# A two-layer decoder step on one core: four output blocks half by half, and the next norm's scales behind the first group's products

## The chip, the cores and the metric

The kernel runs on one core of a Trainium2 chip. The metric is the device time of one execution in microseconds (us). The engines are named as in the profile: PE is TensorE (matmuls), PEld its weight load, DVE VectorE, ACT ScalarE, POOL GpSimd and SP SyncE, which here only issues transfers.

## The reference

One inference step of a decoder with two layers, on 576 tokens (a prompt of 512 and 8 samples of 8), model width 1024, hidden width 2816. Each layer has three sublayers, and every sublayer lies between two RMS norms:

```
x += 0.5 * post_f1(SwiGLU_1(pre_f1(x)))
x += post_m(mixer(pre_m(x) @ W_in) @ W_out)
x += 0.5 * post_f2(SwiGLU_2(pre_f2(x)))
rmsnorm(x, g) = x * rsqrt(mean(x*x) + EPS) * g
```

The mixer of layer 0 ("even") is a gated delta rule beside a short convolution, that of layer 1 ("odd") is sparse attention over a paged cache beside a gated MLP. Outputs are x and the new states and cache rows.

## The kernel before

Activations lie transposed: model rows on 128 partitions in KC = 8 chunks, tokens along the columns, in two halves: half 0 has 256 columns, half 1 has 320 (HALF, HW). Every weight and every activation is split into a high and a low part in the type fp32r (`split`, L98: the high part is a cast on ACT, L101, the low part a subtraction on DVE, L102), and one product of a 128x128 weight block takes three matmuls (`mm3`, L118): whi with the high activation (L119), whi with the low (L120), wlo with the high (L121). Weights come in tiles of eight blocks, 512 KB (`weight`, L105): a transfer on the SP queue into one of three raw buffers, then the split.

The order of the sublayers is ffn(0,0), even, ffn(0,1), ffn(1,0), odd, ffn(1,1). The instructions of each engine stand in an order that the framework's scheduler makes from the program's order; each engine works its list in that order, and an instruction that waits holds all that stand behind it.

**A feed-forward sublayer** (`ffn`, L281) goes over the hidden width in two parts of 11 blocks. For each hidden block it makes the gate and the up product (8 chunks of `mm3`) for half 0 and then half 1. These use x that is not yet divided by its norm: since the scale of a token is a factor of its column, DVE multiplies it in when it takes the products out of PSUM (t, L316, and u, L317: product times r). Then come silu (ACT, L318), the product u*t and its split into hh and hl. After the 11 blocks comes the down projection: eight output blocks `mb` for each half, 33 matmuls each, in the order of `self.out_order`: the blocks 0 to 5 alternate between the halves, the blocks 6 and 7 come first for half 0 and then for half 1. In the second part DVE adds each product to y (L344), ACT squares y (L186) and DVE sums the squares (L187) for the post norm (`y_done`, L245). The mixers end likewise with `proj_out`, 24 matmuls for each output block.

**The seam between two sublayers** is `boundary(hf)` (L209), which runs when a half's last output block is done. `rstd` (L155) makes the scales of the post norm: matmuls of the summed squares with ones (PE, L161, result in the PSUM kind psm), a square root (ACT, L163 and L166), a reciprocal (DVE, L167 and L169), transposes that spread them over the partitions (PE, L173). Then, over the eight chunks, DVE makes bt = y * scale (L227) and adds it to x (L229, or L231 for the last two), ACT writes xh (L195) and DVE xl (L196) for the next sublayer, ACT squares x (L186), POOL adds the squares (L187), and x is stored (L239). From the sum on POOL comes the scale r of the next sublayer's norm by the same `rstd`, with a copy of the result to SBUF (ACT, L177).

**The first group of a sublayer** (`group`, L123) is four products: gate and up of the first two hidden blocks, or the first four blocks of a mixer's input projection. For half 0 it goes product by product, for half 1 chunk by chunk through all four. PSUM has eight banks, three of the kind g, three m and two f; `bank` (L93) hands out the g and f banks in turn, so that five products can be open. A bank is free again when DVE has multiplied its product by r. The scale r of half 0 is made at the end of its boundary; that of half 1 before the last chunk of its first group:

```
later = lambda: self.rstd(accx, w, 1.0 / D, EPS, f"r{hf}")
return later if hf else later()
```

In `odd`, 24 indirect transfers on POOL's queue gather pages of the cache (gcmp, L833, 16 times, and gsel, L858, 8 times); the first is issued after the last sum of squares of the boundary (`issue_after(self.last.ins)`).

Of the kernel before, what the change touches and what calls it, by code (L numbers as in the profile page):

```python
# [16 lines left out]
P = 128  # L17
# [21 lines left out]
class Step:  # L39
    def __init__(self, ctx, tc, a, o):  # L40
        self.tc, self.nc, self.a, self.o = tc, tc.nc, a, o
        self.n = 0
        self.turn = 0
        self.const = ctx.enter_context(tc.tile_pool(name="const", bufs=1))
        self.res = ctx.enter_context(tc.tile_pool(name="res", bufs=1))
        self.wp = ctx.enter_context(tc.tile_pool(name="wp", bufs=4))
        self.ps = ctx.enter_context(tc.tile_pool(name="ps", bufs=4, space=PSUM))
        nc = self.nc
        self.dram = ctx.enter_context(tc.tile_pool(name="dram", bufs=2, space=bass.MemoryType.DRAM))
        self.xd = [a["xT"][:, :, c0:c1] for c0, c1 in HALF]  # L50
        self.g = self.const.tile([P, 12, KC], F32, name="g")
        nc.scalar.dma_start(self.g, a["gT"])
        self.ident = self.const.tile([P, P], F32, name="ident")
        nc.scalar.dma_start(self.ident, a["ident"])
        self.ones = self.const.tile([P, P], F32, name="ones")
        nc.vector.memset(self.ones, 1.0)
        self.biases = {}
        self.small = {}
        self.out_order = [(mb, hf) for mb in range(KC - 2) for hf in range(2)]
        self.out_order += [(mb, hf) for hf in range(2) for mb in range(KC - 2, KC)]  # L60
# [44 lines left out]
    def weight(self, src, inner=P, pool=None):  # L105
        nc = self.nc
        pool = pool or self.wp
        shape = [P, 8 * P // inner, inner]
        raw = self.wp.tile(shape, F32, tag="raw", name=self.nm("raw"), bufs=3)
        bufs = 4 if pool is self.wp else 2  # L110
        hi = pool.tile(shape, F32R, tag="whi", name=self.nm("whi"), bufs=bufs)
        lo = pool.tile(shape, F32R, tag="wlo", name=self.nm("wlo"), bufs=bufs)
# [10 lines left out]
    def group(self, ws, act, rs, hf):  # L123
# [7 lines left out]
        for k in range(KC):  # L131
            if k == KC - 1:
                rs[hf] = rs[hf]()
            for (whi, wlo), p in zip(ws, ps):
                self.mm3(p[:, :w], whi[:, k, :], wlo[:, k, :], act[0][hf][:, k, :], act[1][hf][:, k, :], k == 0, k == KC - 1)
        return ps
# [8 lines left out]

    def new_act(self):
        hi, lo = [], []
        for hf in range(2):
            hi.append(self.res.tile([P, KC, HW[hf]], F32R, tag=f"xh{hf}", name=self.nm("xh")))
            lo.append(self.res.tile([P, KC, HW[hf]], F32R, tag=f"xl{hf}", name=self.nm("xl")))  # L150
        return hi, lo
# [57 lines left out]
    def boundary(self, hf, y, x, acc_y, gpost, c, gnext, act):  # L209
# [4 lines left out]
        accx = self.acc_tile("x") if gnext is not None else None  # L214
# [25 lines left out]
        if gnext is not None:  # L240
            self.xd[hf] = xd
            later = lambda: self.rstd(accx, w, 1.0 / D, EPS, f"r{hf}")
            return later if hf else later()
# [40 lines left out]
    def ffn(self, l, f, act, rs, gpost, gnext, first=None):  # L284
        nc, a = self.nc, self.a
        with ExitStack() as ctx:
# [4 lines left out]
            nact, nrs = None, [None, None]  # L291
            rs = list(rs)
            hp.tile([P, 16], F32, tag="pad", name=self.nm("pad"))
            for part in range(2):
# [27 lines left out]
                if part == 1:  # L322
                    x = self.load_x(yp)
# [5 lines left out]
                def block(n):  # L329
                    t = n // 8  # L330
                    if t not in tiles:
                        tiles[t] = self.weight(a["wdn"][l, f, part, t], pool=yp if part == 1 and t >= 9 else None)
                    return tiles[t][0][:, n % 8, :], tiles[t][1][:, n % 8, :]

                for mb, hf in self.out_order:
# [7 lines left out]
                        else:  # L343
# [4 lines left out]
                            if mb == KC - 1:  # L348
                                if nact is None and gnext is not None:
                                    nact = self.new_act()  # L350
# [4 lines left out]
    def proj_out(self, wsrc, oact, order, gpost, gnext):  # L355
        nc = self.nc
        with ExitStack() as ctx:
# [1140 lines left out]
```

## Time and profile before

| | |
|---|---|
| Median of 3 runs | 2463.08 us (2462.32 to 2464.12) |
| Profiled execution: its own time | 2465.13 us |
| Profiled execution: span of the profile | 2463.4 us |
| PE busy | 2409.8 us, 98% of the span |
| DVE, ACT, POOL busy | 51%, 38%, 7% |
| Mean granted clock of PE | 0.986 |

An engine's busy time is the time in which it has an instruction at work. The waits name the releaser: the instruction whose end let the waiting one start. "issue" means that the profile shows nothing that the engine waited for, "remote" that the releaser is not known. In a timeline the columns are the start, the duration, the engine, the line, the operation, the tile written and those read, the shape, how many instructions the row joins, and in brackets the idle time before it with its releaser. Neighbouring matmuls overlap, so a matmul's price is the distance of two starts, not its duration.

### The profile page before, as it was taken

How to read it: one execution, taken by the hardware profiler on the slowest of the kernel's cores; microseconds unless marked ns; L12 is line 12 of the kernel's file. 1: busy time of each engine (PE TensorE's matmuls, PEld its weight loads, DVE VectorE, ACT ScalarE, POOL GpSimd, SP SyncE). 2: the span in 40 equal slices, each digit the busy share in tenths (PEclk: the TensorE clock that was granted, in tenths of full speed). 3: DMA queues.
4: the chain of work that ended last, by engine and by line, in shares of the span. 5: the costliest groups of instructions: out<-in, count | busy, mean ns of one | idle time of the engine just before them, and what ended most of it. 6: DMA issues, size and time to landing. Idle time of an engine off the chain costs nothing.

```text
span 2463.4 us, 43370 instructions
## 1 busy us (share of the span) xinstructions
PE 2409.8 (98%) x18169; PEld 2318.4 (94%) x18169; DVE 1246.4 (51%) x2489; ACT 926.6 (38%) x1727; POOL 170.9 (7%) x259
## 2 busy tenths in 40 slices
PE   8999999999999999999999999998999999999998
PEld 8999999898999999999999999997866799999997
DVE  5432444777755743244474324445547646423444
ACT  5222334554324522233353223343336645222332
POOL 1000000300001200000020000006002001000000
PEclk9999999999999999999999999999889999999999
DMA  6222222301113322222332222225312123222221
GB/s 224 86 86 78 86 88 95 110 32 63 59 61 140 128 87 86 78 86 86 103 137 86 79 77 94 86 87 183 122 35 75 61 78 137 86 86 78 86 86 56
DMA packets 70323, 226.72 MB, mean 92 GB/s; under 512 B 11136, under 2 KB 17568, under 8 KB 70096
## 3 DMA queue, kind: packets, MB, share of 16 engines
q1 hardware_dynamic: 64288, 204.27, 23.9%
q0 software_dynamic: 5552, 19.57, 2.4%
q8 instruction: 143, 2.34, 0.4%
q14 instruction: 52, 0.43, 0.1%
q10 hardware_dynamic: 288, 0.11, 0.0%
HBM read 204.26 MB, written 20.72 MB: 91 GB/s over the span
## 4 chain that ended last, share of the span: by engine, by line
PE 76%; issue 17%; DVE 5%; ACT 1%; another core or an unknown queue 1%; DMA 1%; POOL 0%; POOLq 0%; DVEq 0%; SPq 0%; ACTq 0%
PE psg L119 14%; PE psg L120 14%; PE psg L121 14%; PE psf L121 8%; PE psf L120 8%; PE psf L119 8%; PE psm L1206 1%; PE psm L494 1%; PE psm L516 1%; PE psf L1248 1%; DVE xl L196 1%; PE psg L1235 1%; PE psm L514 1%; DVE x L229 1%
## 5 line engine op out<-in xcount | busy, mean ns | idle before, releaser
L119 PE MATMUL psg<-xh,whi 128*128 128x256 f32 (+1 forms) x2464 | 734.0, 298 | 11.8 <-ACT xh L195 8.3
L120 PE MATMUL psg<-xl,whi 128*128 128x256 f32 (+1 forms) x2464 | 733.5, 298 | 6.8 <-DVE xl L196 5.2
L121 PE MATMUL psg<-xh,wlo 128*128 128x256 f32 (+1 forms) x2464 | 730.3, 297 | 0.9 <-issue 0.8
L102 DVE TENSOR_TENSOR wlo<-raw,whi 128x1024 fp32r<-128x1024 f32 x330 | 405.2, 1228 | 351.5 <-ACT whi L101 350.0
L101 ACT CAST whi<-raw 128x1024 fp32r<-128x1024 f32 x330 | 345.4, 1050 | 569.2 <-PE psg L120 344.4
L119 PEld LDWEIGHTS psg<-xh,whi 128*128 128x128 f32 x2464 | 467.5, 190 | 14.5 <-ACT xh L195 9.1
L120 PEld LDWEIGHTS psg<-xl,whi 128*128 128x128 f32 x2464 | 466.6, 189 | 14.1 <-DVE xl L196 8.5
L121 PEld LDWEIGHTS psg<-xh,wlo 128*128 128x128 f32 x2464 | 466.7, 189 | 3.9 <-issue 3.0
L120 PE MATMUL psf<-xl,whi 128*128 128x320 f32 (+1 forms) x1280 | 375.8, 294 | 1.5 <-DVE xl L196 1.3
L119 PE MATMUL psf<-xh,whi 128*128 128x320 f32 (+1 forms) x1280 | 375.9, 294 | 0.5 <-ACT xh L195 0.3
L121 PE MATMUL psf<-xh,wlo 128*128 128x320 f32 (+1 forms) x1280 | 375.4, 293 | 0.3
L119 PE MATMUL psg<-hh,whi 128*128 128x256 f32 (+1 forms) x836 | 245.6, 294 | 0.0
L120 PE MATMUL psg<-hl,whi 128*128 128x256 f32 (+1 forms) x836 | 245.2, 293 | 0.0
L121 PE MATMUL psg<-hh,wlo 128*128 128x256 f32 (+1 forms) x836 | 245.1, 293 | 0.0
L120 PEld LDWEIGHTS psf<-xl,whi 128*128 128x128 f32 x1280 | 240.3, 188 | 2.6 <-DVE xl L196 2.2
L119 PEld LDWEIGHTS psf<-xh,whi 128*128 128x128 f32 x1280 | 240.5, 188 | 1.2 <-ACT xh L195 0.5
L121 PEld LDWEIGHTS psf<-xh,wlo 128*128 128x128 f32 x1280 | 240.4, 188 | 0.9 <-DVE wlo L102 0.9
L119 PE MATMUL psf<-hh,whi 128*128 128x320 f32 (+1 forms) x572 | 169.3, 296 | 0.0
L120 PE MATMUL psf<-hl,whi 128*128 128x320 f32 (+1 forms) x572 | 169.0, 295 | 0.0
L121 PE MATMUL psf<-hh,wlo 128*128 128x320 f32 (+1 forms) x572 | 168.8, 295 | 0.0
L101 ACT CAST hh<-u 128x320 fp32r<-128x320 f32 (+1 forms) x176 | 75.9, 433 | 245.7 <-DVE u L319 245.7
L187 POOL TENSOR_TENSOR acc<-acc,sq 128x320 f32<-128x320 f32 (+1 forms) x77 | 70.3, 913 | 1388.8 <-ACT sq L186 1357.7
(467 smaller groups left out, 3173.0 us busy)
## 6 DMA issues: line engine op xcount, KB each, us to landing
raw<-in_wgu SPq DMA_DIRECT2D x176, 512.0 KB
raw<-in_wdn SPq DMA_DIRECT2D x88, 512.0 KB
raw<-in_w_ein SPq DMA_DIRECT2D x28, 512.0 KB
raw<-in_w_oin SPq DMA_DIRECT2D x14, 512.0 KB
xd<-x SPq DMA_DIRECT2D x10, 640.0 KB
x<-xd POOLq DMA_DIRECT2D x10, 640.0 KB
xd<-x SPq DMA_DIRECT2D x10, 512.0 KB
x<-xd POOLq DMA_DIRECT2D x10, 512.0 KB
```

The costliest lines, as they stand in the source:

```text
L101: first = nc.scalar.copy(hi, src)
L102: nc.vector.tensor_tensor(lo, src, hi.bitcast(F32), ALU.subtract)
L119: mm(out, whi, ahi, start=first, stop=False)
L120: mm(out, whi, alo, start=False, stop=False)
L121: mm(out, wlo, ahi, start=False, stop=last)
L187: return (eng or nc.vector).tensor_tensor(acc[:, :w], acc[:, :w], sq[:, :w], ALU.add)
L196: nc.vector.scalar_tensor_tensor(lo, xs, g, hi.bitcast(F32), ALU.mult, ALU.subtract)
L229: (nc.gpsimd if gnext is None and hf and k == 0 else nc.vector).tensor_tensor(xs, xs, t, ALU.add)
L494: nc.tensor.matmul(pz[:w, i * w:i * w + w], m[:, i, :], x[:, i, :], start=True, stop=True)
L514: nc.tensor.matmul(pr[:, 1, i, :], xt[:, i, :], zt[:, i, :], start=True, stop=True)
L516: nc.tensor.matmul(pr[:, 0, i, :], zt[:, i, :], xt[:, i, :], start=True, stop=True)
L1206: nc.tensor.matmul(S[g][:, 0:L], qq[gd, j, P * i:P * i + P], kk[gd, 0:L], start=True, stop=True)
```

## The change

Five things change.

1. `out_order` is now a function. In the second part of a feed-forward sublayer and in `proj_out` the output blocks 0 to 3 alternate between the halves, and the blocks 4 to 7 come first for half 0, then for half 1. In the last sublayer half 1 is ahead of half 0, so that half 0 is the last to end. The first part of a feed-forward sublayer, behind which there is no seam, alternates throughout (`in_turn`).
2. Since the down blocks 4 to 7 are now used for half 0 and again, later, for half 1, their weights stay longer: the tiles from 7 on have buffers of their own, two in the pool yp, two in the space of the next sublayer's xh and xl of half 1 (`spare`). In `proj_out` four weights have buffers of their own rather than two.
3. `boundary` gives the making of r back for both halves, and `group` calls it after all products of the half's first group, for both halves.
4. The sum of squares of half 0's x uses the buffers of accy.
5. The pad in the feed-forward pool grows from 64 to 192 bytes per partition.

The number of matmuls is the same.

```diff
-        self.out_order = [(mb, hf) for mb in range(KC - 2) for hf in range(2)]
-        self.out_order += [(mb, hf) for hf in range(2) for mb in range(KC - 2, KC)]
+        self.in_turn = [(mb, hf) for mb in range(KC) for hf in range(2)]
+
+    def out_order(self, last):
+        halves = (1, 0) if last else (0, 1)
+        return [(mb, hf) for mb in range(KC - 4) for hf in halves] + [(mb, hf) for hf in halves for mb in range(KC - 4, KC)]
...
-    def weight(self, src, inner=P, pool=None):
+    def weight(self, src, inner=P, pool=None, bufs=2, dst=None):
...
+        if dst:
+            hi, lo = dst
+        else:
+            bufs = bufs if pool else 4
+            hi, lo = [(pool or self.wp).tile(shape, F32R, tag=t, name=self.nm(t), bufs=bufs) for t in ("whi", "wlo")]
...
         for k in range(KC):
-            if k == KC - 1:
-                rs[hf] = rs[hf]()
             for (whi, wlo), p in zip(ws, ps):
                 self.mm3(p[:, :w], whi[:, k, :], wlo[:, k, :], act[0][hf][:, k, :], act[1][hf][:, k, :], k == 0, k == KC - 1)
+        rs[hf] = rs[hf]()
         return ps
...
+    def spare(self):
+        flat = [t.rearrange("p k c -> p (k c)")[:, 16:16 + 2 * KC * P].rearrange("p (i s c) -> p i s c", i=2, c=P)
+                for t in self.half_act(1)]
+        return [[t[:, i] for t in flat] for i in range(2)]
...
-        accx = self.acc_tile("x") if gnext is not None else None
+        accx = self.acc_tile("x" if hf else "y") if gnext is not None else None
...
             later = lambda: self.rstd(accx, w, 1.0 / D, EPS, f"r{hf}")
-            return later if hf else later()
+            return later
...
-            hp.tile([P, 16], F32, tag="pad", name=self.nm("pad"))
+            hp.tile([P, 48], F32, tag="pad", name=self.nm("pad"))
...
-                        tiles[t] = self.weight(a["wdn"][l, f, part, t], pool=yp if part == 1 and t >= 9 else None)
+                        pool, dst = None, None
+                        if part == 1 and t >= 7:
+                            pool, dst = (yp, None) if t < 9 else (None, kept[t - 9])
+                        tiles[t] = self.weight(a["wdn"][l, f, part, t], pool=pool, dst=dst)
...
-                for mb, hf in self.out_order:
+                for mb, hf in self.out_order(gnext is None) if part else self.in_turn:
...
-            for mb, hf in self.out_order:
+            for mb, hf in self.out_order(False):
                     if mb not in ws:
-                        ws[mb] = self.weight(wsrc[mb], pool=hp if mb >= KC - 2 else None)
+                        ws[mb] = self.weight(wsrc[mb], pool=hp if mb >= KC - 4 else None, bufs=4)
```

What moves on the engines is shown at three places. The names: psg, psf and psm are PSUM banks, x_12474 and xl_13227 belong to half 1, rcol holds the square roots and their reciprocals. Line numbers of the changed kernel are higher by 5 to 13: its L170, L176, L182, L196, L205, L236, L238, L240, L325, L326 and L357 are the L161, L167, L173, L187, L196, L227, L229, L231, L316, L317 and L344 of the kernel before.

**PE, the seam from ffn(0,1) to ffn(1,0).** Before, the transposes of half 0's r stand in the second product of half 0's first group:

```order
L121 MATMUL psg_13378<-xh_13086,wlo_13337 128x256
L119 MATMUL psg_13378<-xh_13086,whi_13336 128x256
L173 MATMUL psm_13162<-ident,rcol_13157 128x128 x2
L120 MATMUL psg_13378<-xl_13087,whi_13336 128x256
L161 MATMUL psm_13243<-ones,acc_12563 128x1 x2
L161 MATMUL psm_13243<-ones,acc_12563 64x1
```

In the changed kernel they stand behind all four products, five matmuls into half 1's first group:

```order
L126 MATMUL psf_13413<-xh_13004,wlo_13334 128x256
L170 MATMUL psm_13438<-ones,acc_13015 128x1 x2
L124 MATMUL psf_13465<-xh_13226,whi_13315 128x320
L125 MATMUL psf_13465<-xl_13227,whi_13315 128x320
L126 MATMUL psf_13465<-xh_13226,wlo_13316 128x320
L124 MATMUL psf_13465<-xh_13226,whi_13315 128x320
L125 MATMUL psf_13465<-xl_13227,whi_13315 128x320
L182 MATMUL psm_13444<-ident,rcol_13439 128x128 x2
L126 MATMUL psf_13465<-xh_13226,wlo_13316 128x320
```

The sums of half 1's post norm, psm_13243 before, stand in the changed kernel 14 matmuls into the first product of half 0.

**DVE, the same seam.** Before, the reciprocal for r of half 0 (rcol_13157) stands ahead of half 1's boundary, and the evacuations t and u stand within it:

```order
L167 RECIPROCAL rcol_13157<-rcol_13157 128x2
L187 TENSOR_TENSOR acc_12563<-acc_12563,sq_13240 128x320
L316 TENSOR_TENSOR t_13403<-psg_13353,r_13165 128x256
L317 TENSOR_TENSOR u_13404<-psg_13378,r_13165 128x256
L167 RECIPROCAL rcol_13244<-rcol_13244 128x2
L169 RECIPROCAL rcol_13244<-rcol_13244 64x1
L227 TENSOR_TENSOR bt_13258<-y_9004,psm_13252 128x640
L227 TENSOR_TENSOR bt_13269<-y_9004,psm_13252 128x640
L229 TENSOR_TENSOR x_12474<-x_12474,bt_13258 128x640
L316 TENSOR_TENSOR t_13461<-psg_13411,r_13165 128x256
```

In the changed kernel that reciprocal (rcol_13439) is the last but one of half 1's boundary, and t and u follow:

```order
L205 SCALAR_TENSOR_TENSOR xl_13227<-x_12474,g,xh_13226 128x320
L240 SCALAR_TENSOR_TENSOR x_12474<-bt_13289,g,x_12474 128x320
L176 RECIPROCAL rcol_13439<-rcol_13439 128x2
L205 SCALAR_TENSOR_TENSOR xl_13227<-x_12474,g,xh_13226 128x320
L325 TENSOR_TENSOR t_13449<-psg_13338,r_13447 128x256
L325 TENSOR_TENSOR t_13457<-psg_13388,r_13447 128x256
L326 TENSOR_TENSOR u_13450<-psg_13363,r_13447 128x256
L326 TENSOR_TENSOR u_13458<-psf_13413,r_13447 128x256
```

Between the reciprocal of half 1's post norm and this one stand 18 instructions, all of half 1's boundary.

**DVE, the end of the kernel.** Before, half 1's boundary, with columns of 320, is the last (one of its additions is on POOL and not in this list):

```order
L169 RECIPROCAL rcol_25605<-rcol_25605 64x1
L227 TENSOR_TENSOR bt_25617<-y_21418,psm_25613 128x640
L227 TENSOR_TENSOR bt_25621<-y_21418,psm_25613 128x640
L227 TENSOR_TENSOR bt_25625<-y_21418,psm_25613 128x640
L229 TENSOR_TENSOR x_24888<-x_24888,bt_25621 128x640
L229 TENSOR_TENSOR x_24888<-x_24888,bt_25625 128x640
L227 TENSOR_TENSOR bt_25629<-y_21418,psm_25613 128x320
L227 TENSOR_TENSOR bt_25633<-y_21418,psm_25613 128x320
L231 SCALAR_TENSOR_TENSOR x_24888<-bt_25629,g,x_24888 128x320
L231 SCALAR_TENSOR_TENSOR x_24888<-bt_25633,g,x_24888 128x320
```

In the changed kernel half 0's is the last, with columns of 256 and all of it on DVE:

```order
L176 RECIPROCAL rcol_25601<-rcol_25601 128x2
L236 TENSOR_TENSOR bt_25609<-y_21400,psm_25606 128x2x256
L236 TENSOR_TENSOR bt_25613<-y_21400,psm_25606 128x2x256
L238 TENSOR_TENSOR x_24881<-x_24881,bt_25609 128x512
L238 TENSOR_TENSOR x_24881<-x_24881,bt_25613 128x512
L236 TENSOR_TENSOR bt_25617<-y_21400,psm_25606 128x2x256
L236 TENSOR_TENSOR bt_25621<-y_21400,psm_25606 128x256
L238 TENSOR_TENSOR x_24881<-x_24881,bt_25617 128x512
L240 SCALAR_TENSOR_TENSOR x_24881<-bt_25621,g,x_24881 128x256
L236 TENSOR_TENSOR bt_25625<-y_21400,psm_25606 128x256
L240 SCALAR_TENSOR_TENSOR x_24881<-bt_25625,g,x_24881 128x256
```

Half 1's boundary there is ahead of half 0's four last blocks.

## Rows read from the trace of the kernel before

**Rows 1.** The page: span, busy time of each engine.

```profile
PE 2409.8 (98%) x18169; PEld 2318.4 (94%) x18169; DVE 1246.4 (51%) x2489; ACT 926.6 (38%) x1727; POOL 170.9 (7%) x259
```

**Rows 2.** Waits of PE, whole span: total us, times, longest us.

```profile
PE psg L119 <- ACT xh L195: 8.3, 5, 6.0
...
PE psg L120 <- DVE xl L196: 5.2, 10, 1.1
...
PE psm L161 <- POOL acc L187: 1.3, 4, 0.4
PE psf L120 <- DVE xl L196: 1.3, 3, 0.9
PE psg L76 <- DVE pc L436: 1.2, 1, 1.2
```

**Rows 3.** Timeline of PE, the seam from ffn(0,1) to ffn(1,0).

```profile
1242.15 0.28 PE L119 MATMUL psg<-xh,whi 128*128 128x256 f32 x1
...
1243.56 0.28 PE L119 MATMUL psg<-xh,whi 128*128 128x256 f32 x1
...
1251.41 0.71 PE L161 MATMUL psm<-ones,acc 128*128 128x1 f32 x6
1253.43 0.58 PE L173 MATMUL psm<-ident,rcol 128*128 128x128 f32 x3
```

**Rows 4.** Timeline of DVE, the same seam.

```profile
1254.05 1.55 DVE L227 TENSOR_TENSOR bt<-y,psm 128x640 f32<-128x640 f32 x2 [0.67 <-PE psm L173]
...
1262.97 0.54 DVE L196 SCALAR_TENSOR_TENSOR xl<-x,g,xh 128x320 fp32r<-128x320 f32 x1
...
1264.52 1.17 DVE L196 SCALAR_TENSOR_TENSOR xl<-x,g,xh 128x320 fp32r<-128x320 f32 x1
1265.60 0.54 DVE L231 SCALAR_TENSOR_TENSOR x<-bt,g,x 128x320 f32<-128x320 f32 x1
```

**Rows 5.** Timeline of PE, the first group of the kernel.

```profile
24.87 0.42 PE L119 MATMUL psg<-xh,whi 128*128 128x320 f32 x1 [1.01 <-DVE t L316]
```

**Rows 6.** Timeline of PE, the end of the kernel.

```profile
2449.06 0.31 PE L119 MATMUL psg<-hh,whi 128*128 128x320 f32 x1
...
2449.79 0.31 PE L121 MATMUL psg<-hh,wlo 128*128 128x320 f32 x1
2451.87 0.78 PE L161 MATMUL psm<-ones,acc 128*128 128x1 f32 x6 [1.76 <-DVE acc L187]
```

**Rows 7.** Timeline of DVE, the end of the kernel.

```profile
2443.98 1.28 DVE L227 TENSOR_TENSOR bt<-y,psm 128x512 f32<-128x512 f32 x2 [1.82 <-PE psm L173]
...
2448.64 0.48 DVE L344 TENSOR_TENSOR y<-psg,y 128x320 f32<-128x320 f32 x1
2449.04 0.48 DVE L231 SCALAR_TENSOR_TENSOR x<-bt,g,x 128x256 f32<-128x256 f32 x1
...
2454.00 1.55 DVE L227 TENSOR_TENSOR bt<-y,psm 128x640 f32<-128x640 f32 x2 [0.72 <-PE psm L173]
...
2459.47 1.01 DVE L231 SCALAR_TENSOR_TENSOR x<-bt,g,x 128x320 f32<-128x320 f32 x2
```

**Rows 8.** Stretches of the odd start: PE busy (matmuls), PEclk and DMA share among them.

```profile
1705.00:1735.00 30.00, 18.36 (x89) 15.74 (x89) 5.79 (x8) 2.83 (x4) 15.50 (x17) 0.72 0.62 203
1735.00:1740.00 5.00, 5.00 (x41) 5.00 (x40) 2.54 (x5) 3.70 (x6) 0.00 (x0) 1.00 0.06 11
```

**Rows 9.** Timeline of PE, first matmul of `odd`.

```profile
1665.34 0.28 PE L119 MATMUL psg<-xh,whi 128*128 128x256 f32 x1
```

**Rows 10.** Timeline of POOL, the odd start.

```profile
1691.79 1.03 POOL L833 DMA_INDIRECT gcmp<-in_cmp_pool,idx  x1 [0.17 <-issue]
...
1723.24 1.47 POOL L858 DMA_INDIRECT gsel<-in_sel_pool,idx  x1 [0.30 <-issue]
```

**Rows 11.** Timeline of POOL, the seam of rows 3 and 4.

```profile
1258.25 2.92 POOL L187 TENSOR_TENSOR acc<-acc,sq 128x320 f32<-128x320 f32 x3 [9.48 <-ACT sq L186]
1263.35 1.98 POOL L187 TENSOR_TENSOR acc<-acc,sq 128x320 f32<-128x320 f32 x2 [2.18 <-ACT sq L186]
```

More of the change, by code (lines that the diff above doesn't have):

```diff
@@ L103, in split @@
         return first
-    def weight(self, src, inner=P, pool=None):
+    def weight(self, src, inner=P, pool=None, bufs=2, dst=None):
         nc = self.nc
-        pool = pool or self.wp
         shape = [P, 8 * P // inner, inner]
         raw = self.wp.tile(shape, F32, tag="raw", name=self.nm("raw"), bufs=3)
-        bufs = 4 if pool is self.wp else 2
-        hi = pool.tile(shape, F32R, tag="whi", name=self.nm("whi"), bufs=bufs)
-        lo = pool.tile(shape, F32R, tag="wlo", name=self.nm("wlo"), bufs=bufs)
+        if dst:
[3 more added lines that the diff above has]
+            hi, lo = [(pool or self.wp).tile(shape, F32R, tag=t, name=self.nm(t), bufs=bufs) for t in ("whi", "wlo")]
         nc.sync.dma_start(raw, src)
@@ L144, in behind, with half_act @@
         return self.tc.issue_after(inst.ins) if inst else nullcontext()
+    def half_act(self, hf):
+        return [self.res.tile([P, KC, HW[hf]], F32R, tag=f"x{s}{hf}", name=self.nm("x" + s)) for s in "hl"]
     def new_act(self):
[L147 to L151, printed above, removed]
+        return [list(t) for t in zip(*[self.half_act(hf) for hf in range(2)])]
+    def spare(self):
+        flat = [t.rearrange("p k c -> p (k c)")[:, 16:16 + 2 * KC * P].rearrange("p (i s c) -> p i s c", i=2, c=P)
+                for t in self.half_act(1)]
+        return [[t[:, i] for t in flat] for i in range(2)]
     def rstd(self, acc, w, scale, eps, tag, bank="m"):
@@ L290, in ffn @@
             accy = [None, None]
-            nact, nrs = None, [None, None]
+            nact, nrs = [[None, None], [None, None]], [None, None]
             rs = list(rs)
-            hp.tile([P, 16], F32, tag="pad", name=self.nm("pad"))
+            hp.tile([P, 48], F32, tag="pad", name=self.nm("pad"))
             for part in range(2):
@@ L322, in ffn @@
                 if part == 1:
+                    kept = self.spare()
                     x = self.load_x(yp)
@@ L348, in ffn @@
                             if mb == KC - 1:
-                                if nact is None and gnext is not None:
-                                    nact = self.new_act()
+                                if gnext is not None:
+                                    nact[0][hf], nact[1][hf] = self.half_act(hf)
                                 nrs[hf] = self.boundary(hf, y, x, accy[hf], gpost, 0.5, gnext, nact)
```

## The prediction

> **What bounds the kernel now.** I read the page first: PE is busy for 2409.8 us of a span of 2463.4, DVE 51% [rows 1]. The number of matmuls stays, so the change can only give or take PE's idle time, some 50 us. Next the waits of PE, to see which idle time a seam owns: the first products of a sublayer wait for xh (8.3 us, of which one wait of 6.0 is the kernel's start, so 2.3), for xl (5.2 and 1.3) and for the sum on POOL (1.3) [rows 2]. Together 2.3 + 6.5 + 1.3 = 10.1 us, some 2 us at each of the five seams. Then the timelines of one seam on PE and DVE, to see how far DVE's boundary is behind PE; then the end of the kernel, where PE is done and DVE still works; last the start of `odd`, where PE loses the most in one place.
>
> **The change, part by part.** The sum is made against the profiled execution, 2465.13 us; the median of the runs is 2463.08, so I take 2.05 off at the end.
>
> *Half by half, removed.* A matmul of 256 columns costs 0.1175 us (12 starts in 1.41, [rows 3]), one of 320 columns 0.146 (5 starts in 0.73, [rows 6]). Behind half 0's last down block PE now has four blocks of half 1, 4 x 33 x 0.146 = 19.3 us, where it had two, 9.6. In a mixer it is four times 24 rather than two. Half 0's boundary has its xh and xl ready before PE asks, since the waits to be covered are 0.6 to 1.1 us each and the new cover is 7 to 9.6 us longer. So the 10.1 us go. What is late next is half 1.
>
> *The scale of half 0, moved.* On DVE its reciprocal now stands behind half 1's whole boundary but one xl. Take the end of half 1's last block as zero. From the last matmul of a half to its first bt it was 2454.00 - 2450.10 = 3.9 us at the end of the kernel [rows 6, 7]. From that bt to the end of the last addition of x it was 1266.14 - 1254.05 = 12.1 us [rows 4]; two evacuations were among that and one xl (0.54 to 1.17) was not, which about cancel. So the reciprocal is due at 16.0 and the transposes some 0.2 later. PE gets there after four products of half 0, 4 x 24 x 0.1175 = 11.3; the ones-matmuls and transposes of half 1's post norm, 0.71 + 0.58 [rows 3]; four ones-matmuls for half 0, two thirds of 0.71, so 0.5; and five matmuls at 0.146, 0.7: at 13.8. PE then waits 2.4 us and all matmuls of half 1's group are queued behind. This is the upper end. The lower is 0: the xl of half 1 takes 0.54 us undisturbed and 1.17 beside an addition on POOL [rows 4], and if four of seven are undisturbed, 2.5 us go. I take 1.5 a seam, since the old chain also carried evacuations that fed other waits, and because half 1's boundary now begins with DVE less laden.
>
> *Banks held.* Until r of half 0 is there, its four products hold four of five banks, so half 1's first product runs in the fifth and the other three wait for t and u. After the transposes come nine matmuls of that product (1.3 us), about what the copy of r and the first t need. That the wait can exist is seen at the kernel's start, where the first group waits 1.01 us for t [rows 5]. I add nothing for half 0. For half 1, r is now made behind all the products, where 12 matmuls (one chunk of four products, 12 x 0.146 = 1.8 us) used to stand behind it; one product of 256 columns, 2.8 us, is left as cover. Bounds 0 and 1.8; I take 0.7. The five seams so cost 5 x (1.5 + 0.7) = 11.0 and give 10.1: **+0.9**, with ends of 5 x 0 - 10.1 = -10.1 and 5 x 4.2 - 10.1 = +10.9. The first group of the kernel has half 1's part too: **+0.7**.
>
> By the Trainium skill, SBUF — State Buffer, section "Who interferes with whom", a DVE instruction with two SBUF inputs and a GpSimd instruction that reads SBUF lock each other out for the whole instruction. Seven additions of half 1 at 0.98 us (five took 2.92 + 1.98 us, [rows 11]) would then put 6.9 us on an undisturbed chain. The trace bears it out in part: an xl grows by 0.63 us, less than an addition's length; and the 12.1 us above were measured with these additions beside them, so the sum holds what they cost.
>
> *Even's first group.* PE waits 1.2 us for pc at the small projection that follows the group [rows 2]; the group's evacuations now come later on DVE. Bounds 0 and 2.4 (a whole wait for the reciprocal); I take **+0.8**.
>
> *The end.* Half 0 is last. Half 1's boundary took from 2454.00 to 2460.48, 6.5 us; half 0's from 2443.98 to 2449.52 with an evacuation of 0.4 us in it, so 5.1 [rows 7]. The chain up to the first bt loses a reciprocal and a transpose, some 0.2. Gain 1.4 + 0.2: **-1.6**. Half 1's own boundary is under the four blocks of half 0, 4 x 33 x 0.1175 = 15.5 us, of which it needs 3.9 + 6.5. If evacuations of half 0 queue behind it, the gain shrinks to 0.8.
>
> *The start of odd.* Between 1705 and 1735 us PE did 89 matmuls; at the 41 in 5 us of the stretch behind, these are 10.9 us of work in 30, so 19 us are lost [rows 8]. It lies beside the 24 gathers on POOL, 1691.79 to 1724.71 [rows 10], which start behind the boundary's last sum. That was 26.5 us after the first matmul of `odd` [rows 9, 10]; now the reciprocal is due at 16.0 and the last sum some 2 later, so the gathers start about 8.5 us earlier. If the loss ends with the gathers and starts when it did, 8.5 us are gained; if it moves with them, nothing; if they meet more transfers, it grows, by no more than 4 (a fifth of 19). I take **-2.5**, nearer to no change, since the gathers are as long as before.
>
> *Nothing.* The weights' own buffers, the pad and the shared accy buffer add no instruction; the transfers of weights keep their number and order, and DVE is at 51% [rows 1]. If the spare buffers came free too late, casts would be late and PE would show waits for whi, which it has hardly any of now.
>
> Sum: 0.9 + 0.7 + 0.8 - 1.6 - 2.5 = -1.7 us. 2465.13 - 1.7 - 2.05 = 2461.4 us.
>
> **Rivals.** *A, the gathers decide.* The odd start gives the 8.5 us in full. For it: the loss ends within some 10 us of the last gather [rows 8, 10]. Against: the loss begins 13 us after the first. Time: 2461.4 - 6.0 = 2455.4.
>
> *B, the stalls go and nothing takes their place.* DVE is through half 1's boundary before PE needs r. For it: the xl at 0.54 us in rows 4. Against: it needs 2.4 us a seam less than the rows give. Seams -10.1, start 0, even 0, end -1.6, odd 0: 2463.08 - 11.7 = 2451.4.
>
> *C, slower: the reciprocal behind half 1's boundary.* PE stands at the transposes for the full 2.4 us and half 1's late r costs 1.3 at each seam, while odd gives nothing. For it: the distance of 16.0 to 13.8 is from rows alone; DVE has casts of weights to do there as well, which would only lengthen it. Against: it takes the upper end of every bound at once. Seams 5 x 3.7 - 10.1 = +8.4, start +0.7, even +0.8, end -1.6: +8.3, so 2471.4. It decides from a cost of 3.0 us a seam: 15.0 - 10.1 - 0.1 = +4.8.
>
> *D, the change does nothing at the seams.* The scheduler puts the moved work where it costs what it cost. For it: it places ones-matmuls and transposes among products by itself. Only the end counts: 2461.5 to 2463.1.
>
> **How the numbers follow.** A measurement of this kernel can tell a difference of 0.2%, 4.9 us, from none. Chances: the forecast 0.46 (its own range 2456 to 2467, of which 0.06 lies below 2458.2), A 0.21, B 0.12, C 0.16, D 0.05. Faster 0.06 + 0.21 + 0.12 = 0.39; same 0.40 + 0.05 = 0.45; slower 0.16. The range leaves out the lower half of B and the upper part of C: 2451.5 to 2470.
>
> **What the new profile would show.** PE's waits for xl and xh at L195 and L196 (now L204 and L205) near zero outside the kernel's start; in their place a wait of the transposes L182 for rcol of 1 to 2 us at each seam, and short waits of L124 for t. DVE: the reciprocal of half 0 directly before the last xl. At the end 8 to 9 us from the last block to DVE's last instruction, where it was 10.4. In `odd` the gathers from about 18 us after the first matmul. I am wrong if the transposes wait over 3 us (C) or not at all (B), or if the stretch of `odd` with few matmuls has another length than 15 to 20 us of loss (A).

## The result, and the profile after

The changed kernel takes 2486.81 us (median of 4 runs, 2484.65 to 2488.79); the kernel before, run beside it on the same chip, 2463.6 us. The ratio is 1.0085, 95% interval 1.0073 to 1.0097: slower, and above the upper end of the range. The profiled execution took 2488.04 us with a span of 2486.3, 22.9 more than before.

The page after, busy times:

```profile
PE 2418.1 (97%) x18169; PEld 2331.6 (94%) x18169; DVE 1244.4 (50%) x2489; ACT 923.7 (37%) x1725; POOL 164.9 (7%) x259
```

Against [rows 1] PE has as many matmuls and 8.3 us more busy time; the rest is idle. The waits of PE, whole span (total us, times, longest us):

```profile
PE psf L124 <- ACT whi L105: 13.0, 1, 13.0
PE psm L182 <- DVE rcol L176: 10.4, 6, 3.4
PE psg L124 <- ACT xh L204: 6.2, 1, 6.2
...
PE psm L170 <- DVE acc L196: 5.5, 3, 2.7
...
PE psg L80 <- DVE pc L449: 2.7, 1, 2.7
...
PE psg L125 <- DVE xl L205: 2.1, 3, 0.8
PE psg L124 <- DVE t L325: 1.5, 2, 1.0
```

The waits for xh and xl are gone apart from the kernel's start (6.2) and `even` [rows 2]. New are the transposes L182 behind rcol, the ones-matmuls L170 behind DVE's sum, and one wait of 13.0 us for a weight, at the start of `odd`.

PE and then DVE at the seam from ffn(0,1) to ffn(1,0), whose first matmul starts at 1245.78 (compare [rows 3, 4]):

```profile
1259.48 0.30 PE L125 MATMUL psf<-xl,whi 128*128 128x320 f32 x1
1262.98 0.66 PE L182 MATMUL psm<-ident,rcol 128*128 128x128 f32 x2 [3.20 <-DVE rcol L176]
...
1263.97 0.47 PE L125 MATMUL psf<-xl,whi 128*128 128x320 f32 x1
1264.24 0.47 PE L126 MATMUL psf<-xh,wlo 128*128 128x320 f32 x1
```

```profile
1249.71 1.55 DVE L236 TENSOR_TENSOR bt<-y,psm 128x640 f32<-128x640 f32 x2 [0.65 <-PE psm L182]
...
1253.85 2.32 DVE L205 SCALAR_TENSOR_TENSOR xl<-x,g,xh 128x320 fp32r<-128x320 f32 x2
...
1262.68 0.15 DVE L176 RECIPROCAL rcol<-rcol 128x2 f32<-128x2 f32 x1
```

DVE reaches half 0's reciprocal 16.9 us after half 1's last block; PE stood ready at 14.0. Behind the wait the matmuls start 0.27 us apart rather than 0.146. The stretches behind this seam, and behind the seam to ffn(1,1), show why; the column before DMA's share is the granted clock:

```profile
1262.98:1266.40 3.42, 3.42 (x14) 3.42 (x15) 2.56 (x7) 3.21 (x7) 1.91 (x3) 0.50 0.55 208
...
2048.00:2054.80 6.80, 6.80 (x30) 6.32 (x31) 3.75 (x8) 1.54 (x5) 0.00 (x0) 0.50 0.00 0
```

PE is at its lower level, 1.2 GHz, for 3.4 us, or 6.8. The same is seen for 3.4 us at 822.7 and at 1693.1. (Behind the seam to `even` the level is low for 6.8 us in both kernels, from 436.2 before and 447.2 after.) The PE waits at the other seams:

```profile
820.36 0.81 PE L170 MATMUL psm<-ones,acc 128*128 128x1 f32 x6 [1.28 <-DVE acc L196]
836.97 0.40 PE L182 MATMUL psm<-ident,rcol 128*128 128x128 f32 x2 [1.69 <-DVE rcol L176]
...
1692.37 0.40 PE L182 MATMUL psm<-ident,rcol 128*128 128x128 f32 x2 [3.42 <-DVE rcol L176]
...
2047.96 1.26 PE L170 MATMUL psm<-ones,acc 128*128 128x1 f32 x6 [2.73 <-DVE acc L196]
2065.86 0.40 PE L182 MATMUL psm<-ident,rcol 128*128 128x128 f32 x2 [1.30 <-DVE rcol L176]
```

The start of `odd`, by a stretch [rows 8], and the rows of PE, POOL, ACT and DVE there [rows 9, 10]:

```profile
1705.00:1735.00 30.00, 9.33 (x49) 8.32 (x48) 4.50 (x8) 3.67 (x6) 15.06 (x18) 0.60 0.33 104
```

```profile
1674.94 0.28 PE L124 MATMUL psg<-xh,whi 128*128 128x256 f32 x1
...
1729.34 0.58 PE L124 MATMUL psf<-xh,whi 128*128 128x256 f32 x1 [12.95 <-ACT whi L105]
```

```profile
1694.20 1.03 POOL L846 DMA_INDIRECT gcmp<-in_cmp_pool,idx  x1 [0.16 <-issue]
...
1723.63 0.94 POOL L871 DMA_INDIRECT gsel<-in_sel_pool,idx  x1 [0.30 <-issue]
```

```profile
1728.24 2.00 ACT L105 CAST whi<-raw 128x1024 fp32r<-128x1024 f32 x2 [34.96 <-remote]
```

```profile
1729.32 1.23 DVE L106 TENSOR_TENSOR wlo<-raw,whi 128x1024 fp32r<-128x1024 f32 x1 [34.59 <-ACT whi L105]
```

The gathers start 19.3 us after the first matmul of `odd` (26.5 before) and last 30.4 us (32.9 before). PE does 49 matmuls in the 30 us that held 89 before, in a stretch that lies 9.6 us earlier in `odd` than it did there. ACT stands from 1693.3 until 3.7 us after the last gather.

The end, PE and DVE [rows 6, 7]:

```profile
2474.75 0.28 PE L126 MATMUL psg<-hh,xl 128*128 128x256 f32 x1
2476.55 0.58 PE L170 MATMUL psm<-ones,acc 128*128 128x1 f32 x4 [1.52 <-DVE acc L196]
```

```profile
2482.99 0.48 DVE L240 SCALAR_TENSOR_TENSOR x<-bt,g,x 128x256 f32<-128x256 f32 x1
```

From the end of the last block to DVE's end it is 8.4 us, where it was 10.4.

Where the 22.9 us lie, by the starts of the first matmul of each stretch in PE's timeline:

| Stretch | Before | After | Difference |
|---|---|---|---|
| ffn(0,0) part 0, with the start | 222.38 | 219.14 | -3.2 |
| part 1 products of the four feed-forward sublayers | 551.04 | 558.10 | +7.1 |
| `even` with its first group | 280.12 | 282.00 | +1.9 |
| first groups of ffn(0,1), ffn(1,0), ffn(1,1), with the rest of their part 0 and the end of a mixer ahead | 593.63 | 604.64 | +11.0 |
| `odd` with its first group | 310.26 | 318.29 | +8.0 |
| last down projection to the end of the span | 84.22 | 82.41 | -1.8 |

The down projections between them are equal to 0.1 us. The first row differs as much between two executions of the changed kernel (212.98 and 216.87 without the start), so it tells nothing. The 11.0 of these two executions are the new waits, 1.28 + 1.69 + 3.20 + 2.73 + 1.30 = 10.2, less some 2 a seam that went, 6, and half of 3.4 + 3.4 + 6.8 us at the lower clock, 6.8.

The +7.1 hold no wait at all. The same product in part 1 of ffn(0,1), before and then after:

```profile
1100.10 0.28 PE L121 MATMUL psg<-xh,wlo 128*128 128x256 f32 x1
...
1101.46 0.28 PE L121 MATMUL psg<-xh,wlo 128*128 128x256 f32 x1
```

```profile
1100.15 0.28 PE L126 MATMUL psg<-xh,wlo 128*128 128x256 f32 x1
...
1101.56 0.28 PE L126 MATMUL psg<-xh,wlo 128*128 128x256 f32 x1
```

Twelve starts take 1.36 us before and 1.41 after: 113 and 118 ns a matmul of 256 columns. I call these the short and the long rhythm. (The kernel before has the long one too, in its down projections; new is that it holds in the part 1 products.)

### The profile page after: what moved, and what is told of

Its sections match the earlier page's. It is cut to its first block, busy times and chain, and to the rows that moved or that the text cites. A ratio compares the mean times of both kernels' runs of the same rounds, so it can differ in the third digit from the quotient of the medians.

```text
span 2486.3 us, 43395 instructions
## 1 busy us (share of the span) xinstructions
PE 2418.1 (97%) x18169; PEld 2331.6 (94%) x18169; DVE 1244.4 (50%) x2489; ACT 923.7 (37%) x1725; POOL 164.9 (7%) x259
## 4 chain that ended last, share of the span: by engine, by line
PE 74%; DVE 4%; another core or an unknown queue 1%; ACT 1%; issue 1%; DMA 0%; SPq 0%; ACTq 0%; DVEq 0%
PE psg L124 14%; PE psg L125 14%; PE psg L126 14%; PE psf L124 7%; PE psf L125 7%; PE psf L126 7%; PE psm L1219 1%; DVE xl L205 1%; PE psm L507 1%; PE psf L1261 1%; PE psm L529 1%; PE psg L1248 1%; PE psm L527 1%; DVE x L238 1%
## 5 line engine op out<-in xcount | busy, mean ns | idle before, releaser
L124 PE MATMUL psg<-xh,whi 128*128 128x320 f32 (+1 forms) x2464 | 735.7, 299 | 10.2 <-ACT xh L204 6.2
L125 PE MATMUL psg<-xl,whi 128*128 128x320 f32 (+1 forms) x2464 | 732.4, 297 | 2.1 <-DVE xl L205 2.1
L126 PE MATMUL psg<-xh,wlo 128*128 128x320 f32 (+1 forms) x2464 | 732.4, 297 | 0.0
L106 DVE TENSOR_TENSOR wlo<-raw,whi 128x1024 fp32r<-128x1024 f32 x322 | 393.8, 1225 | 398.6 <-ACT whi L105 398.1
L125 PE MATMUL psg<-hl,whi 128*128 128x320 f32 (+1 forms) x766 | 226.7, 296 | 0.0
L124 PE MATMUL psg<-hh,whi 128*128 128x320 f32 (+1 forms) x766 | 226.7, 296 | 0.0
L126 PE MATMUL psg<-hh,wlo 128*128 128x320 f32 (+1 forms) x766 | 226.4, 296 | 0.0
L196 POOL TENSOR_TENSOR acc<-acc,sq 128x320 f32<-128x320 f32 (+1 forms) x77 | 68.6, 891 | 1353.7 <-ACT sq L195 1241.0
L124 PE MATMUL psf<-hh,whi 128*128 128x256 f32 (+1 forms) x514 | 150.2, 292 | 0.0
L126 PE MATMUL psf<-hh,wlo 128*128 128x256 f32 (+1 forms) x514 | 150.2, 292 | 0.0
L125 PE MATMUL psf<-hl,whi 128*128 128x256 f32 (+1 forms) x514 | 150.1, 292 | 0.0
```

The costliest lines, as they stand in the source:

```text
L106: nc.vector.tensor_tensor(lo, src, hi.bitcast(F32), ALU.subtract)
L124: mm(out, whi, ahi, start=first, stop=False)
L125: mm(out, whi, alo, start=False, stop=False)
L126: mm(out, wlo, ahi, start=False, stop=last)
L196: return (eng or nc.vector).tensor_tensor(acc[:, :w], acc[:, :w], sq[:, :w], ALU.add)
```

## The experiments

Runs were made on four chips; each ratio is to the kernel before on the same chip.

**The pad.** e1_pad64 is the changed kernel with the old pad, e2_pad192 the kernel before with the new one.

```diff
-            hp.tile([P, 16], F32, tag="pad", name=self.nm("pad"))
+            hp.tile([P, 48], F32, tag="pad", name=self.nm("pad"))
```

> The changed kernel with the pad at 64 bytes again. In the changed kernel's trace the matmuls of 256 columns run at 117 to 118 ns from start to start in nearly all stretches after 244 us, where in the kernel before those behind the first group of a feed-forward part ran at 113 to 114. Theory 'address': the pad shifts the hidden tiles and sets that rate; then most of the slow stretches become fast again and the time falls by 6 to 10 us, to 2477 to 2481. Rival 'rhythm': the rate is a state of PE that its waits switch, and the pad does nothing: 2487 within 3 us, with the same stretches slow.

> The kernel before with the pad of the change and nothing else. Theory 'address': its fast stretches turn slow, 2463.6 plus 6 to 10 us. Rival 'rhythm': no change, 2463.6 within 3 us.

Measured: e1 1.007 (1.0053 to 1.0087), e2 0.9984 (0.9969 to 0.9999). On this chip too the change costs 0.7%. The part 1 products stay long in e1 (139.21 us each) and short in e2 (137.77, before 137.76). But all of e2's down projections are 1.1 us shorter (68.69 for 69.81, 69.65 for 70.77), seven of them 7.8 us, of which the ratio shows 0.2 to 7.6. The pad is not what costs; in the old order it gives, if by little.

**The scale of half 0 alone.** e3_early_r0 makes it at the boundary's end again; e4_late_scales is the kernel before with both scales late; e5_blocks_only is the changed kernel with both scales where they were.

```diff
 e3: boundary of the changed kernel
-            return later
+            return later if hf else later()
```

> The changed kernel, but half 0's next scale is made at the end of its boundary as before, ahead of half 1's boundary on DVE. Theory 'seam': the waits of the transposes for the reciprocal (10.4 us in six waits in the changed kernel, up to 3.4 us at one seam) go, and the time falls by 8 to 12 us. Rival 'cover': the scale is hidden either way and something else takes those waits: within 3 us of 2487.

> The kernel before with only the scales moved behind the first group's products, for both halves; the output blocks keep their order (two blocks half by half). Theory 'seam': half 0's reciprocal is queued behind half 1's boundary, which starts later against PE than in the changed kernel; the waits of the transposes are as long or longer, 10 to 20 us in all, 2470 to 2483. Rival: the scales cost nothing, 2463.6 within 3 us, and the loss comes from the order of the blocks.

> The changed kernel with all scales made where they were before: the order of the blocks, the buffers and the pad stay. With only half 0's scale moved back the waits for the reciprocal went and PE waited instead 2.6 to 3.1 us at each seam for POOL's sum, with ones-matmuls that stand among half 1's blocks. Theory 'seam moves': that wait stays here, and half 1's earlier scale takes away only the 0.5 us waits for t: ratio 1.004 to 1.007. Rival 'late scales are the loss': ratio 0.998 to 1.002.

Measured: e3 1.0062 (1.0039 to 1.0086), e4 1.0178 (1.016 to 1.0197), e5 1.0068 (1.0044 to 1.0091). The waits of PE that answer, of e3, e4 and e5:

```profile
PE psm L170 <- POOL acc L196: 14.5, 7, 3.1
```

```profile
PE psg L120 <- DVE xl L195: 10.2, 17, 1.4
PE psf L120 <- DVE xl L195: 9.6, 11, 1.4
```

```profile
PE psm L171 <- POOL acc L197: 17.8, 7, 3.1
```

With half 0's scale early its ones-matmuls stand among half 1's four blocks; they wait for POOL's last sum and hold the blocks behind them. With two blocks as cover and the scales late (e4) PE waits for xl instead, and the loss is the largest of all, so the four blocks are worth something to late scales. With four blocks an early scale costs about what a late one does: e3 0.6% against 0.7 for e1 on its chip, e5 0.7% against 0.9 for a1_after on its own, with intervals that overlap.

**Between the two.** e9_r0_second calls half 0's scale behind the second product of its group (half 1's stays behind its group), at a priority that places half 0's reciprocal behind the first bt of half 1's boundary: at ffn(1,0), whose first matmul starts at 1242.48, it comes 5.1 us after half 1's last block, where it was 16.9.

```diff
-            ps = [self.proj(t, act, hf, bank=self.bank()) for t in ws]
-            rs[hf] = rs[hf]()
+            ps = []
+            for n, t in enumerate(ws):
+                ps.append(self.proj(t, act, hf, bank=self.bank()))
+                if n == 1:
+                    with self.urgent(True):
+                        rs[hf] = rs[hf]()
```

> The changed kernel with half 0's next scale made behind the second of its first four products, urgently: its reciprocal then stands on DVE behind the first bt of half 1's boundary, 16 instructions further ahead. Theory 'seam': no wait of the transposes for the reciprocal, no wait for POOL's sum, and the clock stays up at the seams from ffn(0,1) on; 6 to 12 us less than the changed kernel, ratio 1.004 to 1.006. Rival: t and u within half 1's boundary delay its xl by as much, ratio 1.007 or more.

Measured: 0.9999 (0.9981 to 1.0017). DVE at the seam to ffn(1,0), and PE's waits for rcol:

```profile
1247.62 0.16 DVE L180 RECIPROCAL rcol<-rcol 128x2 f32<-128x2 f32 x1
```

```profile
PE psm L186 <- DVE rcol L182: 1.9, 1, 1.9
...
PE psm L186 <- DVE rcol L180: 0.6, 1, 0.6
```

Both are elsewhere (`even` and the end), and at the seam to ffn(1,0) the clock stays at the full level; the ones-matmuls still wait 5.5 us for DVE's sum. The part 0 products of ffn(1,0) take 142.34 us (148.96 and 146.93 in two executions of the changed kernel). `odd` up to its first matmul that reads sel_pair, 664 matmuls of all kinds, takes 113.33 (121.15 and 122.65; the kernel before 114.30). Moving half 0's scale, with the rest of the change as it is, brings the kernel back to the time of the kernel before: its place carries nearly the whole loss. The ratio is the evidence here. The 142.34 alone would not be: with old seams these products took 144.85 us in the profiled execution before, but 147.3 to 149.2 in e2, e6, e7, e10 and e11, where the clock fell at this seam.

**The order of part 0.** e8_part0_order is the changed kernel with part 0's blocks in the old order; e11_part0_in_turn the kernel before with them in turn.

```diff
 e11
-                for mb, hf in self.out_order:
+                for mb, hf in self.out_order if part else [(m, h) for m in range(KC) for h in range(2)]:
```

> The changed kernel with the order of the first part's output blocks as before (two blocks half by half at its end; no seam stands behind it). The part-1 products that follow took 137.8 us each with the old order of blocks and 139.2 to 139.6 in every run with the new one. Theory: the order at the end of the first part sets the rate of the 256-column matmuls behind it; then the part-1 stretches go to 137.8 and the time falls by 5 to 7 us. Rival: the rate comes from elsewhere (the weights' buffers, the second part's order); stretches and time as in the changed kernel, ratio 1.007 to 1.010.

> The kernel before with the first part's output blocks in turn throughout. The converse of the changed kernel with the old order in part 0. Theory: the part-1 stretches of products slow down from 137.8 to 139.2 or more and the kernel by 5 to 7 us, 1.002 to 1.003. Rival: nothing changes, 0.999 to 1.001.

Measured: e8 1.007 (1.004 to 1.0099), e11 1.0024 (1.0011 to 1.0038). In e11 all four part 1 stretches go from 137.76 to 139.21 us, 5.8 of its 6.3 us by the medians. In e8 only the first sublayer is short again (137.77), the others stay at 139.63. So the order alone can switch the rhythm, and something else in the changed kernel does too; what that is was not found.

**The end alone.** e6_tail_only is the kernel before with half 1 first in the last sublayer, two blocks half by half; e7_pad_tail adds the pad; e10_pad_last4 has the pad and, in the last sublayer, four blocks half by half with their buffers.

```diff
 e6
-                for mb, hf in self.out_order:
+                for mb, hf in self.out_order if gnext is not None or part == 0 else [(mb, hf) for mb in range(KC - 2) for hf in (1, 0)] + [(mb, hf) for hf in (1, 0) for mb in range(KC - 2, KC)]:
```

> The kernel before with one thing of the change: in the last sublayer half 1 goes ahead of half 0 (the last two blocks half by half, as before). From last block to the end 8 to 9 us in place of 10.4: 1 to 2 us less, ratio 0.9990 to 1.0000. Rival: the changed order of the last blocks costs at the weights what the shorter boundary gives: 1.000 or above.

> The kernel before with the pad of 192 bytes and half 1 ahead of half 0 in the last sublayer. The pad alone made the down projections 1.1 us shorter in eight stretches and the kernel 0.9984 of before; with the end 0.997 to 0.9985, faster than both kernels. Rival: the order at the end switches the rate back, 0.999 to 1.000.

> The kernel before with the pad of 192 bytes and, in the last sublayer alone, the change's order (four blocks half by half, half 1 first). With two blocks the order at the end gained nothing, since half 0's evacuations stood behind half 1's boundary (PE waited 4.0 us for the sum). With four: last block to the end about 8.2 us, 1 to 2 us less than the pad alone: ratio 0.9970 to 0.9985. Rival: the weights that stay longer come late, or the rate switches: 0.999 or above.

Measured: e6 1.0001 (0.9988 to 1.0013), e7 0.9992 (0.9981 to 1.0004), e10 0.9962 (0.9946 to 0.9978). DVE of e6, then PE's wait of e6 and of e10:

```profile
2454.12 1.01 DVE L231 SCALAR_TENSOR_TENSOR x<-bt,g,x 128x320 f32<-128x320 f32 x2
2455.04 0.75 DVE L344 TENSOR_TENSOR y<-psg,y 128x256 f32<-128x256 f32 x2
```

```profile
PE psm L161 <- DVE acc L187: 4.0, 1, 4.0
```

```profile
PE psm L169 <- DVE acc L195: 1.5, 1, 1.5
```

With two blocks as cover half 0's last evacuations stand behind half 1's boundary, and the gain is lost; with four it is there (8.4 us from the last block to DVE's end). e10 is faster than both kernels. Its interval overlaps e2's: how its gain divides between the pad and the end was not settled. e10 and e7 differ in the last blocks and their buffers alone: from the last down projection to the end e10 takes 82.36 us, e7 85.99.

**The gathers.** e12_after_direct and e13_before_direct read the same number of bytes by plain transfers from the same queue. They read fixed pages and leave out the lookup in the page table, so they do not compute the step; they price the transfers.

```diff
-                        nc.gpsimd.indirect_dma_start(out=gcmp[:, j, :], out_offset=None, in_=a["cmp_pool"],
-                                                     in_offset=bass.IndirectOffsetOnAxis(ap=idx[:, j:j + 1], axis=0))
+                        nc.gpsimd.dma_start(gcmp[:, j, :], a["cmp_pool"][P * j:P * j + P, :])
```

> The changed kernel with each indirect gather of a page replaced by a plain transfer of as many bytes on the same queue (fixed pages, so the lookup in the page table is left out). At the start of odd the changed kernel stood idle until the last gather was through (13 to 18 us for a cast of weights) and took 121 to 123 us for a stretch that ran in 99 us on a chip where no such stop was seen. Theory 'gathers': without indirect transfers the stop goes, the stretch takes 97 to 103 us and the kernel 15 to 22 us less than the changed kernel. Rival 'volume': plain transfers of the same bytes hold the engines as long, within 5 us of the changed kernel.

> The kernel before with the same replacement. Theory 'gathers': its stretch falls from 114 us to 97 to 102, the kernel by 12 to 16 us, and the distance of the changed kernel to this one without gathers is 14 to 18 us (seams, clock and rate alone) where it was 22 with them. Rival 'volume': no change.

Measured on one chip: 0.9992 (0.9974 to 1.001) and 0.9941 (0.9918 to 0.9965). `odd` up to its first matmul with sel_pair takes 98.08 us in both, and e12's wait of 13 us for a weight is gone. ACT's cast waits 12.8 us there, for PE to free the buffer, rather than 35; the waits for rcol stay:

```profile
1700.23 1.99 ACT L105 CAST whi<-raw 128x1024 fp32r<-128x1024 f32 x2 [12.80 <-PE psf L125]
```

```profile
PE psm L182 <- DVE rcol L176: 11.4, 6, 3.7
```

So without the indirect transfers the change costs 0.9992 / 0.9941, 0.5%, of its 0.85%. The other 0.35%, some 8 us, is what the gathers take from the changed kernel beyond the 0.6% that they take from the kernel before. With intervals of 0.2% on either ratio the split is good to some 0.3%.

**The changed kernel again, and a mend.** a1_after is the changed kernel unchanged; e14_r0_part0 is e9 with part 0 in the old order.

> The changed kernel once more, beside the other kernels of this call on their chip. If the rate of the 256-column matmuls belongs to the program, its stretches are the same as in the first trace (part-1 products of the feed-forward sublayers 139.6 us each, down projections 69.8 and 70.8 but for the first); if it is an accident of an execution, other stretches are slow. If the long stop at the start of odd belongs to the chip and not to the program, the gap of 13 us there is gone. Ratio to the kernel before 1.006 to 1.010.

> The changed kernel with half 0's scale behind the second product and the first part's blocks in their old order: both causes undone, the four blocks, the buffers, the pad and the late scale of half 1 kept. With the scale alone it stood at 0.9999 of the kernel before. If the old order in part 0 brings the part-1 stretches back to 137.8 us in all sublayers, 0.997 to 0.998; if in the first one alone, as in the changed kernel with that order, 0.9985 to 0.9995.

Measured: a1 1.0089 (1.0063 to 1.0115), with waits at L182 of 12.8 us in all and one of 17.8 for the weight in `odd`. e14 0.9968 (0.9944 to 0.9992): part 1 is short in the first and the last sublayer, and it is faster than the kernel before. The weights' own buffers and the shared accy buffer are kept in e9 and e14; alone they were not tested.

## Why the prediction was wrong

**Where the sum and the measurement part.** The sum was -1.7 us and the spans differ by +22.9, so 24.6 are to be found. By the stretches of the table, with its +0.9 spread over the five seams, the sum had +0.5 for the three seams to ffn(0,1), ffn(1,0) and ffn(1,1), where 11.0 were measured; -2.3 for `odd` with its seam, where it was 8.0; 0 for the part 1 products, where it was 7.1; and +1.0 for `even`, where it was 1.9. For the kernel's start it had +0.7, where the row of -3.2 tells nothing, and for the end -1.6, where it was -1.8. So three steps failed: the seams, by what was not in the sum; "The start of odd", by its sign; and "Nothing". The term for the scale of half 0 was too low by 2.3 us of the 24.6.

**The scale of half 0, moved: right in mechanism, too low.** Its ends were 0 and 2.4 us a seam, and I took 1.5, "since the old chain also carried evacuations that fed other waits, and because half 1's boundary now begins with DVE less laden". Measured were 1.69, 3.20, 3.42 and 1.30 at the four seams behind `even`, a mean of 2.4, and 0.2 at `even`: 9.8 us for 7.5. The upper end came from rows; what I set against it came from none. The chain's parts were nearly right: first bt at 3.9 us (forecast 3.9), PE at 14.0 (13.8), the reciprocal at 16.9 (16.0). The 0.9 lie between first bt and reciprocal, 13.0 us rather than 12.1: leaving out two evacuations did not make up for the one xl more that was now ahead of it. Beside POOL's sums an xl is dear, 1.16 us (two in 2.32) where one alone takes 0.54. The Trainium skill (SBUF — State Buffer, "Who interferes with whom") says that a DVE instruction with two SBUF inputs contends with a GpSimd one that reads SBUF; the trace agrees, though the xl grows by less than the length of a sum.

**Two terms were not in the sum.** First the ones-matmuls of half 1's post norm, which wait 1.3 and 2.7 us for DVE's sum at the two seams behind a mixer. DVE comes to half 1's last four sums only behind the last xl of half 0's boundary, so it does not begin "less laden":

```profile
2044.63 0.48 DVE L205 SCALAR_TENSOR_TENSOR xl<-x,g,xh 128x256 fp32r<-128x256 f32 x1 [0.58 <-ACT xh L204]
2045.26 2.65 DVE L196 TENSOR_TENSOR acc<-acc,sq 128x320 f32<-128x320 f32 x4
```

Second the clock. PE stood 1.3 to 3.4 us at once where it had stood some 2 a seam in pieces of 0.7 at most, and behind it the rows show the lower level for 3.4 us at three seams and 6.8 at the fourth: half of 17.0, 8.5 us. In the profiled execution of the kernel before the granted clock was 1.00 at these seams. But that is no property of the old seam. The first row is the kernel before; the other two are e11, with the same short waits:

```profile
1242.00:1262.00 20.00, 17.85 (x137) 16.55 (x136) 17.58 (x32) 10.29 (x25) 6.50 (x8) 1.00 0.22 86
```

```profile
1246.35 0.38 PE L119 MATMUL psg<-xh,whi 128*128 128x256 f32 x1 [0.69 <-ACT xh L195]
...
1246.90:1257.10 10.20, 9.98 (x46) 9.20 (x45) 3.61 (x10) 3.16 (x8) 0.64 (x1) 0.50 0.26 90
```

In e2, e6, e7, e10 and e11 the clock is at the lower level for 6.8 or 10.2 us at this seam, behind waits of 0.7 us at most; in e13, with the same waits, it stays up. So the 8.5 us are the difference of two executions, and the change's own share of them is not shown. Over all executions on the chip of a1_after the mean granted clock is 0.985 for the kernel before (21) and 0.983 for the changed one (4), which is some 5 us for the whole kernel.

**Half by half, removed:** right at four of the five seams. At `even` two waits for xl of 0.83 us stay.

**Banks held:** too high; waits for t are 1.5 + 0.5 us in the whole kernel, of which the 0.5 stands behind the seam to ffn(1,0) and the 1.5 ahead of `even`, against 0.7 a seam.

**Even's first group:** +0.8 forecast; the waits for pc are 2.7 and 1.3 where one of 1.2 stood, +2.8.

**The end:** -1.6 forecast, -1.8 measured, by the mechanism named; e6 shows that two blocks do not suffice.

**The start of odd:** the gathers came when forecast (18 us after the first matmul, measured 19.3), and the sign was wrong: -2.5 against a loss. Of the 8.0 us of the stretch some 3.1 belong to its seam (3.42 of wait and half of 3.4 us of clock, less the 2.0 that went), so some 4.9 are left for the gathers, about the "no more than 4" that the forecast gave a loss as bound; e12 and e13 make it some 8, good to some 0.3% of the kernel. I took the loss as a length of time that moves or stays. The rows show a stop that holds until the last gather is through: in the changed kernel the gathers begin when half 1's group has just begun, at 1694.2, and a cast that is next on ACT does not come before 1728.2. That it costs more when less of PE's list is free of it is my reading. e12 and e13 show that the indirect transfers are the cause on their chip; on the chip of e1 to e4 the same gathers run without such a stop. Why a gather holds ACT is argued at the end and not shown.

**Nothing:** wrong by 7.1 us. I costed the pad at zero as it adds no instruction, and the order of part 0 had no term at all; e11 shows 5.8 us from the order alone and e2 some 4 (by its ratio) the other way from the pad. With it fell the first step, that the change "can only give or take PE's idle time": with as many matmuls PE is busy for 8.3 us more.

**Rival C** had the place, the mechanism and the sign, with a chance of 0.16, but not the size: 2471.4 us, 15 below the measured time. Its price, 3.7 us a seam, lacked the ones-matmuls and the clock; and it had nothing for `odd` and the rhythm. It had the sign by half 0's scale, which is the cause that e9 confirms.

## What to carry to other kernels

A scale moved behind PE's work is also moved in the list of the engine that makes it: place the short reciprocal ahead of the long boundary there, as e9 did, and check both lists. A wait on PE can cost more than its length, since the granted clock can fall behind it; but the same waits of 0.7 us cost nothing of the clock in one execution and 3 to 5 us in another, so such a price is taken from more than one execution. Orders and pads that add no instruction are measured alone, since they can switch the rhythm of the matmuls.

## What the runs showed of the hardware

**Two rhythms.** Matmuls of 256 columns run at 113 or 118 ns start to start for whole stretches at the full clock, those of 320 columns at 146.6 in either. The order of blocks that ran earlier (e11), and 128 bytes of pad (e2), switch it. What decides it is open.

**Gathers can stop the engines.** While 24 indirect transfers run, PE, ACT and DVE all stand for a time (13.0, 35.0 and 34.6 us in one piece in the changed kernel). The same cast on ACT waits 12.8 us in e12, without indirect transfers, so not all of the 35.0 is theirs. The transfer queues of the changed kernel between 1686 and 1733.5 us, and of e12 over the same length, 1680 to 1727.5:

```profile
q0 software_dynamic: 1152, 3.15, 21.3%
q1 hardware_dynamic: 717, 2.25, 13.0%
q14 instruction: 2, 0.02, 0.1%
```

```profile
q1 hardware_dynamic: 2663, 7.31, 45.9%
q0 software_dynamic: 1152, 3.15, 19.8%
q8 instruction: 2, 0.03, 0.3%
...
```

The same packets on the software queue, but none of instruction queue q8 for the whole stop. The Trainium skill (Runtime: NRT & Kernel Launch, "Instruction fetch mechanics") says that engines stream their instructions by a transfer queue of their own, at a cost "mostly hidden". That they starved here would fit, and no run shows it: PE starts again at 1729.34, within the stretch without a packet, so the missing packet may as well be what engines that stand leave behind.

**Chips differ.** On one chip the kernel before took 2445.76 us, on the others 2463.6 to 2464.2; there `odd` up to its first matmul with sel_pair took 92.0 to 104.2 us in e1 to e4, with gathers (110 to 123 in the runs with gathers on the others). Why is open.
